# All weight sums of a layer's up projection on Vector instead of GpSimd, with a kept first block, another order of w_o's units and later gate pieces

## The chip, the cores and the metric

The kernel runs on one core of a Trainium2 chip. The metric is the device time of one execution in microseconds (us); the median of the kernel before is 1641.47 us over 3 runs. The engines are TensorE (PE, with its weight loads as PEld), Vector (DVE), Scalar (ACT), GpSimd (POOL) and SyncE (SP), whose queue issues most of the transfers. Each engine runs its instructions in the order of the program.

## The reference

One decoder layer on a sequence of 1024 tokens with 1024 channels, in float32. What matters here is its second half:

```python
x  = LN_1(alpha * x + gate1 * (y @ w_o))                # y: the two mixers, gated
h2 = LN(x) * (1 + scale2) + shift2
u  = h2 @ w_up                                          # 1024 -> 2 * 2816
u  = conv_b + sum(conv_w[t] * pad(u)[:, t:t + S] for t in range(3))   # causal, per channel
f  = gelu(u_gate) * u_val
x  = LN_2(alpha * x + gate2 * (f @ w_down))
```

`gate2` is one part of `SiLU(c) @ w_ada + b_ada`, a vector of 1024 numbers.

## The kernel before, in words

Every float32 operand of a matmul is held as a high and a low part (`hi`, `lo`), and a product is three matmuls (hi*hi, lo*hi, hi*lo). The split is made by two instructions: a CAST on Scalar writes hi (L381), and a subtraction on Vector writes lo (L382). TensorE's order is written by hand. A planner hangs other work between its units: `at(delay, cost, fn)` puts `fn` into a queue, and it is emitted when the planner's clock (in planned us of TensorE work) has passed the delay. The order on each other engine is the order of emission.

The stages, in us of the trace: modulation, first layer norm and the mixers up to about 840; w_o with the two layer norms behind it to about 950; the up projection with its convolution to about 1377; the down projection with the last layer norm to the end.

**w_o.** The work is cut in units `(n, t)`: token tile t of 128 rows, and columns 0-255 (n = 0), 256-511 (n = 1) or 512-1023 (n = 2). A unit is 24 matmuls. Its result goes from PSUM to SBUF by one instruction on Vector, the evacuation (L982). When the last unit of a tile, n = 2, is evacuated, the tile is complete and `ln_tile(t)` follows: `ln_a` is LN_1 (statistics on Vector, L367 and L369; `rs` on GpSimd, L360 and L361; the two passes L1067 and L1068 on Vector), `ln_b` is the statistics of the second norm on Vector, `rs` and `nb` on GpSimd (L360, L361, L377), and the normalisation on Scalar (L1073). Behind tile 3, and again behind tile 7, come eight `h2_part`s each: four transposes on TensorE (L1084), one Scalar pass out of PSUM with the modulation (L1089), then a split into h2's hi and lo.

**The up projection** is done as seven products of blocks instead of eight (Winograd's form of Strassen's rule): h2 is cut in four blocks of 512 tokens by 512 channels, B11, B12, B21 and B22, from which `T1 = B12 - B11`, `T2 = B22 - T1`, `T3 = B22 - B12` and `T4 = B21 - T2` are made on Vector (h2_part, `t1_t3`, `b22_t4`; L1075, L1112, L1115, L1124). The weights come in 22 pairs i of 128 gate channels and 128 value channels. Each pair has four blocks of weights of 128x512 numbers, and four sums of these are made by tensor_tensor instructions: three when `operand` is called for product 6 (L1210 to L1212), one for product 4 (L1216). All four stand on GpSimd:

```python
pool.tensor_tensor(out=r[4], in0=r[2], in1=r[3], op=ALU.add)
pool.tensor_tensor(out=r[2], in0=r[0], in1=r[2], op=ALU.subtract)
pool.tensor_tensor(out=r[0], in0=r[4], in1=r[0], op=ALU.subtract)
```

`operand` is called seven products ahead of its use, and splits the block or sum (names `whi`, `wlo`, from `raw` or `wst`). A product is twelve matmuls (L1265 to L1267) into a bank `pj`, `m` or `w`, and its evacuation adds it to `u` (L1275 on Vector, L1272 a copy on Scalar). Behind a pair's last product come `conv` (L1175 on Scalar, two passes L1177 on Vector, for gate and value each), the GELU (L1184, Scalar), the multiplication (L1185, Vector) and the store to `fd` (SP). The first four pairs run two of their seven products (1 and 2) early, in and between w_o's last units and the transposes.

**The gate.** gate2 is computed on Vector in 36 pieces (`ada3_part`): a load of 128x256 weights and one multiply-add each (L601). The piece number m comes at a planned delay of ADA3_D + ADA3_P * m.

**The down projection** reads `fd` back in 512 columns (`down_prep`), splits it (`fh`, `fl`, or `fe` for the first three blocks) and the weights, and starts with the blocks of `fe` (`f_slot`), which lie in the pool of the convolution's tiles, tag `y`. Its results are evacuated, scaled by gate2 and normalised by `finish`.

Of the kernel before, what the change touches and what calls it, by code (L numbers as in the profile page):

```python
# [9 lines left out]
F32 = mybir.dt.float32  # L10
F32R = mybir.dt.float32r
# [19 lines left out]
PSCALE = 2.0 ** 14  # L31

EARLY = 4
B_FIRST = 3
B_LAST = (3, 5)
MOD_PE = 2
ADA3_D = 70.0
ADA3_P = 8.5
T3_P, T4_P = 2.0, 2.6
ADA_D = 5.0  # L40
ADA_E = 8
# [76 lines left out]
def hybrid_layer_kernel(ctx: ExitStack, tc: tile.TileContext, x, pos, wlra, wbig, wup, wdn, ada1, ada2, cst, pv, sm, lr,  # L118
# [959 lines left out]
    def h2_part(hf, kt):  # L1078

        if h2[hf] is None:  # L1080
            h2[hf] = [hp.tile([P, 4, NK, P], F32R, name=f"h2{hl}", tag="h") for hl in "hl"]
        pt = ps1("m")
        for t in range(4):
            pe.transpose(out=pt[:, t * P:(t + 1) * P], in_=x1[4 * hf + t][:, kt * P:(kt + 1) * P], identity=ident)  # L1084
        if hf == 0:
            f = hq.tile([P, 512], F32, name="xt", tag="raw", bufs=6)
        else:
            f = tmp["b", kt] = t_slot(3 if kt < 4 else 4, "h", kt % 4, F32)
        act.activation(out=f, in_=pt, func=AF.Identity, scale=mods[:, 3][:, kt:kt + 1], bias=mods[:, 2][:, kt:kt + 1])  # L1089
        if hf == 0:  # L1090
            split_to([hl[:, :, kt, :] for hl in h2[0]], rows4(f))
        elif kt < 4:
            t1 = tmp["t1", kt] = t_slot(3, "l", kt, F32)
            b11 = [hl[:, :, kt, :].bitcast(F32) for hl in h2[0]]
            sub(rows4(t1), rows4(f), b11[0])
            sub(rows4(t1), rows4(t1), b11[1])
        else:
            k = kt - 4
            t2 = tmp["t2", k] = t_slot(4, "l", k, F32)
            sub(t2, f, tmp["t1", k])  # L1100
            if k % 2 == 0:
                t2h[0] = hq.tile([P, 2, 512], F32R, name="t2h", tag="t2h", bufs=2)
            tt_[2][k] = t2h[0][:, k % 2, :], t_slot(2, "l", k)
            split_to(tt_[2][k], t2)
# [41 lines left out]
        pe.matmul(pt, lhsT=ones, rhs=gate[:, cs], start=True, stop=True)  # L1146
        act.copy(out=gate[:, cs], in_=pt)

    for n, t in ((2, 0), (1, 4), (2, 1), (1, 5), (2, 2), (1, 6), (2, 3), (1, 7), (2, 4), (2, 5), (2, 6), (2, 7)):
        if n < 2:  # L1150
            wo_unit(n, t)
        else:
            o_unit(t, g_o2, 512, 512, lambda: ln_tile(t))
        if n == 2 and t % 4 == 3:
            for m in range(NK):
                kt = m if t == 3 else m // 2 + 4 * (m % 2)
                at(H2_D + H2_P * m, 0.45, lambda kt=kt, t=t: h2_part(t // 4, kt))
# [35 lines left out]
    def load(i, js=(0, 2, 3, 1)):  # L1193
# [4 lines left out]
            sp.dma_start(r[j], wup[i, j].rearrange("p (k c) -> p k c", k=4))  # L1198
        return r

    def operand(i, p):

        if p < 3 and i < EARLY:
            return pair(load(i, (p - 1,))[p - 1])
        if i not in raws:
            raws[i] = load(i)
        r = raws[i]
        if p == 6:
            r[4] = hq.tile([P, 4, P], F32, name="raw", tag="raw", bufs=6)
            pool.tensor_tensor(out=r[4], in0=r[2], in1=r[3], op=ALU.add)  # L1210
            pool.tensor_tensor(out=r[2], in0=r[0], in1=r[2], op=ALU.subtract)
            pool.tensor_tensor(out=r[0], in0=r[4], in1=r[0], op=ALU.subtract)  # L1212
        if p == 7 and i + 1 < NFF and i + 1 not in raws:
            raws[i + 1] = load(i + 1)
        if p == 4:
            pool.tensor_tensor(out=r[1], in0=r[1], in1=r[0], op=ALU.subtract)  # L1216
        return pair(r[{1: 0, 2: 1, 3: 1, 4: 3, 5: 4, 6: 0, 7: 2}[p]])

    seq = [(0, 1), (1, 1), (0, 2), (1, 2), (2, 1), (3, 1), (2, 2), (3, 2)]
# [64 lines left out]

    def f_slot(s, i):

        if s == 0 and i < B_FIRST:
            e_ = yp.tile([P, 2, 512], F32R, name="fe", tag="y")
            return e_[:, 0, :], e_[:, 1, :]
# [122 lines left out]
```

## Time and profile before

| what | value |
| --- | --- |
| time, median of 3 runs | 1641.47 us (1641.31 to 1641.97) |
| time of the profiled execution | 1640.05 us |
| span of the profiled execution, first to last instruction | 1638.3 us |
| mean granted clock of TensorE in it | 0.987 |
| TensorE busy | 1572.9 us, 96% |
| Vector busy | 1090.7 us, 67% |
| Scalar busy | 746.2 us, 46% |
| GpSimd busy | 470.7 us, 29% |

The span leaves out what lies ahead of the first instruction and behind the last, 1.75 us in this execution. The granted clock is the TensorE clock that the chip allowed, as a share of full speed (2.4 GHz; the lower level is 1.2 GHz), so a stretch at 0.90 ran part of it at the lower level. Busy time is the time in which at least one instruction of the engine runs.

### The profile page before, as it was taken

What the parts mean: (1) busy time and instruction counts of PE and PEld (TensorE: products, weight loads), DVE (VectorE), ACT (ScalarE), POOL (GpSimd) and SP (SyncE); (2) the same over time, 40 slices, a digit from 0 to 9 for tenths busy, and PEclk for the clock granted to TensorE, in tenths of its full rate; (3) what the DMA queues carried; (4) which work ended last, traced back from release to release, by engine and by line L of the source; (5) the groups of instructions that cost most, each with busy time, mean ns of one, the idle gap of its engine ahead of it and who ended that gap; (6) DMA issues with size and microseconds to landing.
All of it is one profiled execution on the core that took longest, in us unless ns stands there. A gap on an engine that the chain in (4) does not pass through costs nothing.

```text
span 1638.3 us, 28077 instructions
## 1 busy us (share of the span) xinstructions
PE 1572.9 (96%) x10542; PEld 1390.8 (85%) x10543; DVE 1090.7 (67%) x2125; ACT 746.2 (46%) x1710; POOL 470.7 (29%) x662
## 2 busy tenths in 40 slices
PE   6999999999999999999999779999999998999997
PEld 5999999998998998989988657778888777888885
DVE  6766666675746555535759799898888877437535
ACT  5665555554544534544423544444444444333430
POOL 2122222222532623515404442333223220003103
PEclk9999999999999999999999889999999999999999
DMA  7500000013114032120244313332222225743641
GB/s 265 159 27 27 28 27 27 28 53 113 60 43 149 26 104 91 31 64 18 65 154 148 104 55 103 105 98 78 77 78 78 79 73 195 250 143 112 203 142 52
DMA packets 79795, 152.87 MB, mean 93 GB/s; under 512 B 8981, under 2 KB 15641, under 8 KB 79658
## 3 DMA queue, kind: packets, MB, share of 16 engines
q1 hardware_dynamic: 79658, 151.07, 28.8%
q8 instruction: 83, 1.36, 0.4%
q14 instruction: 54, 0.44, 0.1%
HBM read 131.11 MB, written 19.92 MB: 92 GB/s over the span
## 4 chain that ended last, share of the span: by engine, by line
PE 79%; DVE 11%; DMA 3%; issue 3%; ACT 2%; POOL 2%; SPq 0%; POOLq 0%; DVEq 0%; ACTq 0%
PE pj L337 10%; PE pj L338 10%; PE pj L339 10%; PE w L1323 7%; PE pj L1323 4%; PE m L1323 3%; PE w L1265 3%; PE w L1267 2%; PE w L1266 2%; DVE cv L1177 2%; PE m L715 2%; PE pj L352 2%; PE m L754 2%; PE pj L353 2%; PE pj L354 2%
## 5 line engine op out<-in xcount | busy, mean ns | idle before, releaser
L337 PE MATMUL pj<-whi,hh 128*128 128x256 f32 (+1 forms) x1296 | 372.6, 287 | 0.1
L339 PE MATMUL pj<-whi,hl 128*128 128x256 f32 (+1 forms) x1296 | 366.2, 283 | 0.0
L338 PE MATMUL pj<-wlo,hh 128*128 128x256 f32 (+1 forms) x1296 | 366.1, 282 | 0.0
L337 PEld LDWEIGHTS pj<-whi,hh 128*128 128x128 f32 x1296 | 247.4, 191 | 0.6 <-issue 0.2
L338 PEld LDWEIGHTS pj<-wlo,hh 128*128 128x128 f32 x1296 | 245.7, 190 | 0.5 <-issue 0.2
L339 PEld LDWEIGHTS pj<-whi,hl 128*128 128x128 f32 x1296 | 245.5, 189 | 0.0
L381 ACT CAST whi<-wst 128x512 fp32r<-128x512 f32 x176 | 107.0, 618 | 150.3 <-PE w L1266 48.4
L382 DVE TENSOR_TENSOR wlo<-wst,whi 128x512 fp32r<-128x512 f32 x176 | 132.5, 763 | 52.4 <-ACT whi L381 52.2
L1177 DVE SCALAR_TENSOR_TENSOR cv<-u,pv_sb,cv 128x1023 f32<-128x1023 f32 x88 | 118.4, 1346 | 10.0 <-ACT cv L1175 10.0
L360 POOL TENSOR_SCALAR rs<-mv 128x1 f32<-128x1 f32 x32 | 15.3, 478 | 329.0 <-DVE mv L1336 245.4
L253 DVE TENSOR_TENSOR wlo<-wst,whi 128x512 fp32r<-128x512 f32 (+1 forms) x108 | 78.1, 742 | 45.7 <-ACT whi L252 45.3
L382 DVE TENSOR_TENSOR fl<-wst,fh 128x512 fp32r<-128x512 f32 x41 | 29.0, 708 | 80.5 <-ACT fh L381 80.5
L381 ACT CAST whi<-raw 128x512 fp32r<-128x512 f32 x66 | 40.9, 620 | 80.3 <-PE m L1266 39.9
L694 POOL TENSOR_SCALAR_AFFINE_SELECT pch<-ph 128x512 f16<-128x512 f16 x32 | 20.5, 642 | 195.5 <-ACT ph L689 195.5
L1210 POOL TENSOR_TENSOR raw<-raw 128x512 f32<-128x512 f32 x22 | 35.5, 1616 | 140.6 <-DMA raw<-in_wup 85.8
L1216 POOL TENSOR_TENSOR wst<-wst 128x512 f32<-128x512 f32 x22 | 36.3, 1651 | 133.4 <-issue 125.4
L252 ACT CAST whi<-wst 128x512 fp32r<-128x512 f32 (+1 forms) x108 | 65.4, 620 | 20.1 <-PE pj L353 10.6
L1265 PE MATMUL pj<-h2h,whi 128*128 128x512 f32 x176 | 71.4, 406 | 1.5 <-DVE y L982 1.5
L1266 PE MATMUL pj<-h2l,whi 128*128 128x512 f32 x176 | 69.9, 397 | 0.0
L1267 PE MATMUL pj<-h2h,wlo 128*128 128x512 f32 x176 | 69.9, 397 | 0.0
L601 DVE SCALAR_TENSOR_TENSOR gate<-aw,csil,gate 128x512 f32<-128x512 f32 (+1 forms) x70 | 57.5, 830 | 17.8 <-DMA aw<-in_ada 17.6
L1266 PE MATMUL m<-h2l,whi 128*128 128x512 f32 x176 | 69.2, 393 | 0.0
(461 smaller groups left out, 4472.2 us busy)
## 6 DMA issues: line engine op xcount, KB each, us to landing
wst<-in_wbig SPq DMA_DIRECT2D x112, 256.0 KB, 3.0
wst<-in_wdn SPq DMA_DIRECT2D x88, 256.0 KB, 3.3
aw<-in_ada SPq DMA_DIRECT2D x80, 256.0 KB, 3.4
wst<-in_wup SPq DMA_DIRECT2D x52, 256.0 KB, 2.6
raw<-in_wup SPq DMA_DIRECT2D x44, 256.0 KB, 2.9
fd<-cv SPq DMA_DIRECT2D x22, 512.0 KB, 4.0
wst<-fd SPq DMA_DIRECT2D x44, 256.0 KB, 3.1
y<-in_x SPq DMA_DIRECT2D x8, 512.0 KB, 8.9
```

The source lines that it names most:

```text
L252: act.copy(out=hi, in_=st)
L253: dve.tensor_tensor(out=lo, in0=st, in1=hi.bitcast(F32), op=ALU.subtract)
L337: pe.matmul(acc, lhsT=lh, rhs=wh, start=kt == 0 if start is None else start, stop=False)
L338: pe.matmul(acc, lhsT=lh, rhs=wl, start=False, stop=False)
L339: pe.matmul(acc, lhsT=ll, rhs=wh, start=False, stop=kt == NK - 1 if stop is None else stop)
L381: act.copy(out=hl[0], in_=src)
L382: dve.tensor_tensor(out=hl[1], in0=src, in1=hl[0].bitcast(F32), op=ALU.subtract)
L1177: dve.scalar_tensor_tensor(out=c_[:, lag:S], in0=u[:, 0:S - lag], scalar=wv[:, 2 - lag:3 - lag], in1=c_[:, lag:S], op0=ALU.mult, op1=ALU.add)
L1265: pe.matmul(acc, lhsT=wh[:, kt, :], rhs=bh, start=p not in (2, 3) and kt == 0, stop=False, **go)
L1266: pe.matmul(acc, lhsT=wh[:, kt, :], rhs=bl, start=False, stop=False, **go)
L1267: pe.matmul(acc, lhsT=wl[:, kt, :], rhs=bh, start=False, stop=kt == 3, **go)
L1323: pe.matmul(acc, lhsT=l_[:, ts_], rhs=r_, start=i == 0 and n == 0, stop=i == NFF - 1 and n == 2)
```

## The change

Five edits, in the order of the diff:

1. All four sums of all 22 pairs are issued on Vector, 88 instructions; GpSimd has none of them.
2. The gate's pieces begin at a planned delay of 130 instead of 70 and follow each other at 7.5 instead of 8.5.
3. For the first four channel blocks, the first half of h2 (B11) is written to slots of its own (tag `t2l`, four slots, later used by T2's low parts) and kept in float32 until T1 is made. T1 is then one subtraction from it; before, it took two, one for B11's high and one for its low part. These four blocks no longer take slots of tag `raw`.
4. The order of w_o's last units.
5. In the down projection's first half the first two blocks `fe` lie in slots of tag `t2h` instead of slots of tag `y`.

```diff
+S_DVE = NFF
...
-ADA3_D = 70.0
-ADA3_P = 8.5
+ADA3_D = 130.0
+ADA3_P = 7.5
...
         if hf == 0:
-            f = hq.tile([P, 512], F32, name="xt", tag="raw", bufs=6)
+            f = (hq.tile([P, 512], F32, name="xt", tag="raw", bufs=6) if kt > 3 else
+                 hq.tile([P, 512], F32, name="t2lf", tag="t2l", bufs=4))
+            tmp["b11", kt] = f
         else:
...
             t1 = tmp["t1", kt] = t_slot(3, "l", kt, F32)
-            b11 = [hl[:, :, kt, :].bitcast(F32) for hl in h2[0]]
-            sub(rows4(t1), rows4(f), b11[0])
-            sub(rows4(t1), rows4(t1), b11[1])
+            sub(t1, f, tmp.pop(("b11", kt)))
...
-    for n, t in ((2, 0), (1, 4), (2, 1), (1, 5), (2, 2), (1, 6), (2, 3), (1, 7), (2, 4), (2, 5), (2, 6), (2, 7)):
+    for n, t in ((2, 0), (2, 1), (2, 2), (1, 4), (2, 3), (1, 5), (2, 4), (1, 6), (2, 5), (1, 7), (2, 6), (2, 7)):
...
+    eng = lambda i: dve if i < S_DVE else pool
+
     def operand(i, p):
...
-            pool.tensor_tensor(out=r[4], in0=r[2], in1=r[3], op=ALU.add)
-            pool.tensor_tensor(out=r[2], in0=r[0], in1=r[2], op=ALU.subtract)
-            pool.tensor_tensor(out=r[0], in0=r[4], in1=r[0], op=ALU.subtract)
+            eng(i).tensor_tensor(out=r[4], in0=r[2], in1=r[3], op=ALU.add)
+            eng(i).tensor_tensor(out=r[2], in0=r[0], in1=r[2], op=ALU.subtract)
+            eng(i).tensor_tensor(out=r[0], in0=r[4], in1=r[0], op=ALU.subtract)
...
         if p == 4:
-            pool.tensor_tensor(out=r[1], in0=r[1], in1=r[0], op=ALU.subtract)
+            eng(i).tensor_tensor(out=r[1], in0=r[1], in1=r[0], op=ALU.subtract)
...
     def f_slot(s, i):
 
+        if s == 0 and i < 2:
+            e_ = hq.tile([P, 2, 512], F32R, name="fe", tag="t2h", bufs=2)
+            return e_[:, 0, :], e_[:, 1, :]
         if s == 0 and i < B_FIRST:
             e_ = yp.tile([P, 2, 512], F32R, name="fe", tag="y")
```

Line numbers of the changed kernel are one higher from the new constant on, two to three higher from `operand` on (L1213 to L1215 and L1219 are the sums, L1278 the evacuation on Vector, L1178 the convolution's passes).

Three places of the program follow as rows of each engine's order.

Vector, from the evacuation of w_o's last unit (2,7) to the second statistics of its tile 7 (`mv<-bst` at the end). Before:

```order
L982 SCALAR_TENSOR_TENSOR y<-xt,pj 128x512
L367 BN_STATS bst<-y 128x6 x3
L369 BN_AGGR mv<-bst 128x2
L367 BN_STATS bst<-y 128x6
L382 TENSOR_TENSOR wlo<-wst,whi 128x512
L369 BN_AGGR mv<-bst 128x2
L601 SCALAR_TENSOR_TENSOR gate<-aw_14571,csil,gate 128x256
L1067 SCALAR_TENSOR_TENSOR y<-y,mv,g1b 128x1024
L1068 SCALAR_TENSOR_TENSOR y<-y,rs,b1b 128x1024
L382 TENSOR_TENSOR wlo<-wst,whi 128x512
L367 BN_STATS bst<-y 128x6 x2
L382 TENSOR_TENSOR wlo<-raw,whi 128x512
```

(the aggregation L369 of tile 7's second statistics is the next row). In the changed kernel:

```order
L983 SCALAR_TENSOR_TENSOR y<-xt,pj 128x512
L368 BN_STATS bst<-y 128x6 x3
L370 BN_AGGR mv<-bst 128x2
L1213 TENSOR_TENSOR raw<-raw 128x512
L1068 SCALAR_TENSOR_TENSOR y<-y,mv,g1b 128x1024
L370 BN_AGGR mv<-bst 128x2
L1214 TENSOR_TENSOR raw<-wst,raw 128x512
L1069 SCALAR_TENSOR_TENSOR y<-y,rs,b1b 128x1024
L1215 TENSOR_TENSOR wst<-raw,wst 128x512
L368 BN_STATS bst<-y 128x6 x2
L383 TENSOR_TENSOR wlo<-wst,whi 128x512
L370 BN_AGGR mv<-bst 128x2
```

Three sums of a pair stand in the chain now, and two splits, one gate piece and the other tile's last statistics row have left it.

GpSimd at the same place, before, where the layer norms' small instructions (`rs`, `nb`) and the sums share one order:

```order
L1210 TENSOR_TENSOR raw<-raw 128x512
L360 TENSOR_SCALAR rs<-mv 128x1
L361 TENSOR_TENSOR rs<-rs,mhalf 128x1
L1211 TENSOR_TENSOR raw<-wst,raw 128x512
L377 TENSOR_SCALAR nb<-mv,rs 128x1
L1212 TENSOR_TENSOR wst<-raw,wst 128x512
L360 TENSOR_SCALAR rs<-mv 128x1
L361 TENSOR_TENSOR rs<-rs,mhalf 128x1
```

In the changed kernel:

```order
L361 TENSOR_SCALAR rs<-mv 128x1
L362 TENSOR_TENSOR rs<-rs,mhalf 128x1
L361 TENSOR_SCALAR rs<-mv 128x1
L362 TENSOR_TENSOR rs<-rs,mhalf 128x1
L378 TENSOR_SCALAR nb<-mv,rs 128x1
```

Only the small ones are left there.

Vector in the up projection, where a pair's products 7, 5 and 4 are evacuated and the next pair's sums are due. Before, one pair's stretch from one evacuation of `m` to the next of `w`:

```order
L1275 TENSOR_TENSOR u<-m,u 128x512
L382 TENSOR_TENSOR wlo<-raw,whi 128x512
L601 SCALAR_TENSOR_TENSOR gate<-aw_15399,csil,gate 128x256
L1275 TENSOR_TENSOR u<-w_14230,u 128x512
L382 TENSOR_TENSOR wlo<-wst,whi 128x512
L601 SCALAR_TENSOR_TENSOR gate<-aw_15463,csil,gate 128x256
L382 TENSOR_TENSOR wlo<-wst,whi 128x512
```

In the changed kernel, some pairs later, where the gate's pieces stand now:

```order
L1278 TENSOR_TENSOR u<-m,u 128x512
L383 TENSOR_TENSOR wlo<-raw,whi 128x512
L1213 TENSOR_TENSOR raw<-raw 128x512
L1278 TENSOR_TENSOR u<-w_14517,u 128x512
L383 TENSOR_TENSOR wlo<-wst,whi 128x512
L1214 TENSOR_TENSOR raw<-wst,raw 128x512
L1215 TENSOR_TENSOR wst<-raw,wst 128x512
L602 SCALAR_TENSOR_TENSOR gate<-aw_15703,csil,gate 128x256
L383 TENSOR_TENSOR wlo<-wst,whi 128x512
```

The first sum L1213, which reads two blocks just loaded, now stands ahead of an evacuation (`u<-w`). On SP a pair's four loads and its store come in the order raw, wst, raw, wst, fd in place of raw, wst, wst, raw, fd.

Scalar between the up and the down projection, up to the cast of the third block `fe`. Before:

```order
L381 CAST fe<-wst 128x512
L381 CAST whi<-wst 128x512 x2
L381 CAST fh<-wst 128x512
L381 CAST whi<-wst 128x512
L1175 ACTIVATE cv<-u,pv_sb 128x1024
L381 CAST whi<-wst 128x512
L381 CAST fh<-wst 128x512
L1175 ACTIVATE cv<-u,pv_sb 128x1024
L381 CAST fe<-wst 128x512
```

In the changed kernel:

```order
L382 CAST fe<-wst 128x512 x2
L382 CAST whi<-wst 128x512
L1275 COPY u<-pj 128x512
L382 CAST whi<-wst 128x512
L1185 ACTIVATE cv<-cv 128x1024
L382 CAST whi<-wst 128x512 x3
L1176 ACTIVATE cv<-u,pv_sb 128x1024
L382 CAST whi<-wst 128x512
L1176 ACTIVATE cv<-u,pv_sb 128x1024
L382 CAST fe<-wst 128x512
```

The first two `fe` are cast together, and the two casts of `fh` that stood ahead of the third are behind it.

## Rows read from the trace of the kernel before

**Rows 1.** The page's first part: busy us, share of the span, instructions.

```profile
PE 1572.9 (96%) x10542; PEld 1390.8 (85%) x10543; DVE 1090.7 (67%) x2125; ACT 746.2 (46%) x1710; POOL 470.7 (29%) x662
```

**Rows 2.** Busy time by stretch: PE, PEld, DVE, ACT, POOL; then clock, DMA share, GB/s.

```profile
852.40:931.60 79.20, 70.20 (x357) 58.00 (x355) 68.15 (x106) 29.05 (x40) 38.85 (x48) 0.97 0.45 148
...
852.40:1000.00 147.60, 126.34 (x572) 101.04 (x571) 132.42 (x189) 64.28 (x94) 59.67 (x59) 0.92 0.33 107
1000.00:1120.00 120.00, 118.34 (x508) 94.64 (x507) 108.58 (x129) 51.76 (x72) 35.73 (x25) 1.00 0.31 102
1120.00:1320.00 200.00, 199.48 (x864) 161.52 (x863) 158.68 (x173) 88.93 (x124) 65.34 (x43) 1.00 0.25 80
...
932.90:994.90 62.00, 49.86 (x198) 38.00 (x196) 59.01 (x79) 32.86 (x53) 18.84 (x10) 0.88 0.18 53
```

**Rows 3.** TensorE's waits from 840 to 1010: us in total, times, longest.

```profile
PE w L1265 <- DVE u L1275: 7.0, 3, 3.3
PE m L1084 <- ACT y L1073: 4.8, 1, 4.8
PE m L1084 <- ACT xt L1089: 2.7, 1, 2.7
PE w L1265 <- ACT t4h L381: 2.2, 1, 2.2
PE w L1266 <- DVE t4l L382: 2.1, 1, 2.1
PE pj L1265 <- DVE y L982: 1.5, 1, 1.5
```

**Rows 4.** TensorE's timeline in w_o: start, us, what; a fast and a slow stretch.

```profile
863.77 0.40 PE L337 MATMUL pj<-t3h,yTh 128*128 128x512 f32 x1
...
904.76 0.63 PE L337 MATMUL pj<-t3h,yTh 128*128 128x512 f32 x1
```

**Rows 5.** Vector's timeline at the first and the last tile of w_o; idle before, releaser.

```profile
852.63 0.69 DVE L982 SCALAR_TENSOR_TENSOR y<-xt,pj 128x512 f32<-128x512 f32 x1 [1.78 <-PE pj L339]
...
914.89 0.68 DVE L982 SCALAR_TENSOR_TENSOR y<-xt,pj 128x512 f32<-128x512 f32 x1
...
923.41 2.31 DVE L1068 SCALAR_TENSOR_TENSOR y<-y,rs,b1b 128x1024 f32<-128x1024 f32 x1 [2.15 <-POOL rs L361]
...
928.03 0.20 DVE L369 BATCH_NORM_AGGREGATE mv<-bst 128x2 f32<-128x12 f32 x1
```

**Rows 6.** GpSimd's timeline at the last tile's second norm.

```profile
928.32 0.94 POOL L360 TENSOR_SCALAR rs<-mv 128x1 f32<-128x1 f32 x1 [3.68 <-DVE mv L369]
```

**Rows 7.** Scalar's timeline, the normalisation of the last tile.

```profile
930.32 1.24 ACT L1073 ACTIVATE y<-y,nb,rs 128x1024 f32<-128x1024 f32 x1 [5.15 <-POOL nb L377]
```

**Rows 8.** Vector's timeline behind the transposes.

```profile
956.15 1.78 DVE L1075 TENSOR_TENSOR xt<-t4hf,t3hf 128x512 f32<-128x512 f32 x1
...
959.56 0.68 DVE L1075 TENSOR_TENSOR xt<-h2h,t4lf 128x512 f32<-128x512 f32 x1
960.16 0.68 DVE L1115 TENSOR_TENSOR t3l<-xt,t3h 128x512 fp32r<-128x512 f32 x1
...
994.27 0.69 DVE L1275 TENSOR_TENSOR u<-w,u 128x512 f32<-128x512 f32 x1
```

**Rows 9.** TensorE's waits from 1000 to 1120.

```profile
PE w L1265 <- DVE u L1275: 1.7, 5, 0.6
```

**Rows 10.** A pair's last load issued by SP, twice, and the sum on GpSimd behind it.

```profile
1174.71 0.33 SPq L1198 DMA_DIRECT2D raw<-in_wup  x1
...
1194.04 0.33 SPq L1198 DMA_DIRECT2D raw<-in_wup  x1
...
1178.45 1.36 POOL L1210 TENSOR_TENSOR raw<-raw 128x512 f32<-128x512 f32 x1 [6.05 <-DMA raw<-in_wup]
```

**Rows 11.** The start of the down projection, Scalar and TensorE.

```profile
1381.62 0.60 ACT L381 CAST fe<-wst 128x512 fp32r<-128x512 f32 x1
...
1382.27 0.80 PE L1323 MATMUL pj<-whi,fe 128*128 128x512 f32 x1 [4.01 <-ACT fe L381]
```

## The prediction

> **What bounds the kernel now.** The page's first part comes first: TensorE is busy for 1572.9 of 1638.3 us, the others far less [rows 1]. So work moved between other engines can gain at most what TensorE loses, about 65 us, and the question is where it loses them and to whom. The busy time by stretch answers the first half. In the convolution's steady part, 1120 to 1320, TensorE is busy 199.48 of 200 us at full clock: nothing is to be gained there. In 1000 to 1120 it loses 1.7 us. From 852.4 to 1000 it is busy 126.34 of 147.6 us and its clock was 0.92 [rows 2]: 21.3 us of waits, and a part of the rest at the lower clock level. This is where the change can act. The view of TensorE's waits names the releasers there: 7.0 us for evacuations on Vector, 4.8 for the normalisation of the last tile on Scalar, 2.7 for the first half's h2 blocks, 2.2 and 2.1 for T4's parts, 1.5 for w_o's last evacuation [rows 3]. The waits are paid twice: a matmul of 512 columns takes 0.40 us before them and 0.63 us behind one [rows 4].
>
> Then I ask what those releasers wait for, and it is Vector each time. From 932.9 to 994.9 Vector is busy 59.01 of 62.0 us, more than TensorE's 49.86 [rows 2]: in this stretch Vector is the bound. Part of that busy time is not its own. The subtraction L1075 on 512 columns took 1.78 us at 956.15, while a sum ran on GpSimd, and 0.68 at 959.56, when none did; alone, such instructions start 0.60 apart [rows 8]. And at w_o's end Vector stood still for 2.15 us until GpSimd had made `rs` [rows 5], which stood behind the sums in GpSimd's order.
>
> **The change part by part.** I sum in four places, from Vector's prices. Unhindered, I count an instruction by the distance of starts: 0.60 us for 512 columns [rows 8], 1.20 for 1024 (twice that), 0.40 for a gate piece and 0.1 for an aggregation (estimates).
>
> *First place, up to the second half's transposes.* From 852.4 until the normalisation ends at 930.32 + 1.24 = 931.6 [rows 7], TensorE is busy 70.2 of 79.2 us at 0.97 of the clock [rows 2]. The idle 9.0 us are the three waits 2.7 + 1.5 + 4.8 [rows 3]; the clock costs 0.03 x 79.2 = 2.4. At full speed without waits TensorE would be there at 931.6 - 9.0 - 2.4 = 920.2. The new unit order puts the units (1,t) between the (2,t), so that tiles complete further apart and the last unit no longer comes as the fourth in a row; I leave 1.5 us of waiting for the blocks in front: 921.7. Does Vector's chain allow that? From its first evacuation (852.63 + 0.6 = 853.2) to the evacuation of (2,7) at 914.89 [rows 5], 61.7 us, the order of before has 86 instructions, 50.7 us unhindered; so 11.0 went to waits and hindrance. The changed order has 85, 50.3 us, since what sums it takes on is offset by gate pieces and splits that went later. I take half of the 11.0, because the hindrance by GpSimd goes and the waits for TensorE stay: 853.2 + 50.3 + 5.5 = 909. From there to tile 7's second aggregation it is 8.7 us with three sums on the way, 1.8 of it; before, it took from 914.89 to 928.03, 13.1 [rows 5], for 9.1 of work. Behind it, GpSimd starts 0.3 us and Scalar 2.3 us later [rows 6, 7]; this remains. So 909 + 8.5 + 2.3 + 1.2 = 921.0, just ahead of TensorE. The gain is 931.6 - 921.7 = **9.9**; the bounds are 0 (the chain stays as late) and 11.4 (no wait, full clock).
>
> *Second place, from there to 995.* Before, Vector needed 62.0 us for 78 instructions up to the evacuation at 994.27 that TensorE awaits [rows 8]. They are 69 of 512 columns, 6 of 1024 and 3 gate pieces: 69 x 0.60 + 6 x 1.20 + 3 x 0.40 = 49.8 us. Ten of them were stretched beyond 0.60 or 1.20 between starts, by 8.6 us together (the row of 956.15 is one: 1.1); the other 3.6 are waits. In the changed order 84 instructions lie in front of that evacuation, 54.8 us: nine sums come (+5.4), the four second subtractions of T1 go (-2.4), a multiplication and a convolution pass that stood behind it now stand in front (+2.4), and a gate piece leaves (-0.4). With the 3.6 of waits, and 1.0 for the sums' waits for their operands, it is 59.4 in place of 62.0. The gain is **2.6**. The bounds: 8.6 of hindrance less 5.0 of work, 3.6, if no new wait arises, and 4.6 more if the old waits go too; and a loss of 5.0, if the hindrance stays or returns as waits.
>
> At this place the Trainium skill (Perfetto Trace Analysis, Optimizing Scalar/DVE Operations) speaks against the change: if DVE is saturated, handing work to Scalar or even GpSimd can make sense, and here work is taken back by a saturated Vector. It adds that the two share a port to SBUF, so that moving work between them might not help. The trace has the first (59.01 of 62.0 us busy) and bears the second out with 1.78 against 0.68 us. By the first alone the second place would lose 5.0, and the time would be near 1634.6; by the second it gains.
>
> *Third place, 1000 to 1120.* TensorE waited 1.7 us, five times, for an evacuation on Vector [rows 9]. There, gate pieces leave (about three per pair went through this stretch) and sums come. I take **1.0**, between 0 and 1.7.
>
> *Fourth place, the start of the down projection.* TensorE waited 4.01 us for the third block's cast, issued at 1381.62 [rows 11]. In the changed order the two casts `fh` stand behind it, and the first two blocks no longer wait for a slot of the convolution's tiles; the cast still waits for a slot and for the convolution's last passes. I take **1.0** and bound it by 0 and 4.0.
>
> *At nothing:* the 88 sums over the rest of the convolution. 18 pairs take 1194.04 - 1174.71 = 19.3 us each [rows 10], set by TensorE. In 1120 to 1320 Vector is busy 158.68 us [rows 2]; with four sums in each of 10.4 pairs, 10.4 x 2.4 = 25, it stays at 184 of 200 at most, and at less as hindrance by GpSimd goes. Gate pieces, about two in a pair for some time, add 0.8 per pair. The cover is TensorE's own 19.3 us; without it each sum would cost 0.6. The later gate is needed only when the first tile of the down projection finishes, some hundred us later. SP's queue issues as many transfers as before.
>
> Sum: 9.9 + 2.6 + 1.0 + 1.0 = 14.5 us. The profiled execution took 1640.05, so 1625.55; the median of the runs shown lies 1.42 higher, which gives **1627.0** us.
>
> **The rivals.**
>
> *Everything hidden by Vector goes* (1614 to 1622). The 5.5, 3.6 and 1.0 us of waits that I left on Vector were partly followers of GpSimd's delays; without them, and with the whole 4.0 at the last place, the gain is 11.4 + 7.2 + 1.7 + 4.0 = 24.3, or 1617. For it: TensorE's waits all hang on one engine, and each wait removed spares lower clock behind it. Against it: the evacuations wait for TensorE as well.
>
> *The first place alone counts* (1632 to 1637). Vector, already the bound behind the transposes, loses with its added work as much as it gains: 9.9 - 5.0 = 4.9, or 1636.6, up to 9.9 and 1631.6 without loss.
>
> *No change* (1638.2 to 1644.8). Three sums stand between the two statistics of the last tile, and each waits for a load. If one is 10 us late, the normalisation is as late as before and the first place gives nothing.
>
> *Slower.* In each pair the first sum stands ahead of the evacuation of `w` in Vector's order and waits for the pair's last load. On GpSimd it began 3.74 us after the issue (1174.71 to 1178.45) [rows 10], where nothing was behind it. Vector's pair without the sums is 7 splits, 5 evacuations and 5 instructions of 1024 columns, 12 x 0.60 + 5 x 1.20 = 13.2 us; with four sums it is 15.6, and with two gate pieces 16.4. Of the 3.74 us I let Vector wait half, 1.9, since it has work in hand for the other half (an estimate). 19.3 - 16.4 - 1.9 = 1.0 is left. So it decides from a landing 4.8 us after issue on; at 6 us each of 18 pairs would be 1.2 us longer, +21.6 against -14.5: 1648.5. Against it: two successive pairs show the same distance, and the changed SP order issues the last `raw` load no later.
>
> **How the numbers follow.** Main case 0.45, with a range of its own of 1622 to 1632; everything goes 0.20; first place alone 0.20; no change 0.08; slower 0.07. A measurement of this kernel can tell about 0.2%, 3.3 us, from no change. Faster by over that holds the first three: 0.85; within it 0.08; slower 0.07. The range of 8 in 10 goes from 1616, which leaves out the lower edge of the second case, to 1637, the upper end of the third: it leaves out the last two cases and a little below.
>
> **What would show it.** First place: the wait for `y` on Scalar in front of the transposes at 1 us or gone, the transposes at about 922, GpSimd's `rs` directly behind the aggregation. Second place: no 512-column instruction on Vector above 0.7 us; the awaited evacuation at about 982. Third: no waits above 0.5 us. Fourth: the wait for `fe` at about 3 us. Steady pairs at 19.3 us, Vector's first sum with a wait of about 2 us. The prediction is wrong if pairs are longer than 19.4, if a sum at w_o's end waits long for its load, or if Vector's waits behind the transposes grow beyond 5 us.

## The result

| what | before | changed |
| --- | --- | --- |
| median of 4 runs | 1641.72 us (1641.31 to 1644.71) | 1624.45 us (1621.93 to 1624.92) |
| profiled execution: time, span | 1640.05, 1638.3 us | 1624.25, 1622.4 us |
| mean granted clock | 0.987 | 0.990 |

The ratio of the times is 0.9888, 95% interval 0.9871 to 0.9905: faster by 17.3 us, where 14.5 us and 1627.0 were forecast. The page's first part of the changed kernel, to be held against [rows 1]:

```profile
PE 1565.8 (97%) x10543; PEld 1388.2 (86%) x10543; DVE 1084.5 (67%) x2209; ACT 745.1 (46%) x1710; POOL 333.6 (21%) x574
```

GpSimd lost 88 instructions and 137 us, Vector gained 84 instructions and yet is busy for 6 us less: its other instructions became shorter by more than the sums cost it. Busy time by stretch, columns as in [rows 2]:

```profile
852.40:921.60 69.20, 68.90 (x351) 57.77 (x351) 61.39 (x103) 25.25 (x35) 26.10 (x38) 0.97 0.47 158
...
1000.00:1120.00 120.00, 120.00 (x521) 97.55 (x520) 105.84 (x146) 54.34 (x75) 0.00 (x0) 1.00 0.28 93
1120.00:1320.00 200.00, 200.00 (x868) 162.73 (x867) 166.81 (x227) 88.37 (x123) 0.00 (x0) 1.00 0.27 87
```

TensorE has next to no idle time in front of the transposes (busy 68.90 of 69.20 us), and none from 1000 to 1320. Its waits from 835 to 1000, columns as in [rows 3]:

```profile
PE w L1268 <- DVE u L1278: 9.2, 3, 5.9
PE w L1268 <- ACT t4h L382: 2.0, 2, 1.8
...
PE m L1085 <- ACT y L1074: 1.2, 1, 1.2
PE w L1269 <- DVE t4l L383: 0.9, 2, 0.6
PE m L1085 <- ACT t4hf L1092: 0.3, 1, 0.3
PE m L1085 <- ACT t2lf L1092: 0.3, 1, 0.3
```

The waits in front of the transposes, 2.7 us for the first half's blocks (the row with `t2lf` now) and 4.8 for `y`, are 0.3 and 1.2 now, and that for w_o's last evacuation is gone. The waits for Vector's evacuations behind the transposes are not shorter but longer, 9.2 in place of 7.0 us, and the longest of all the stage is one of them, 5.9 us.

The last tile's chain: Vector, GpSimd, Scalar, TensorE in the timeline of the changed kernel, to be held against [rows 5 to 7].

```profile
911.79 0.67 DVE L983 SCALAR_TENSOR_TENSOR y<-xt,pj 128x512 f32<-128x512 f32 x1
...
920.60 0.69 DVE L383 TENSOR_TENSOR wlo<-wst,whi 128x512 fp32r<-128x512 f32 x1 [0.82 <-ACT whi L382]
921.21 0.20 DVE L370 BATCH_NORM_AGGREGATE mv<-bst 128x2 f32<-128x12 f32 x1
...
921.50 0.55 POOL L361 TENSOR_SCALAR rs<-mv 128x1 f32<-128x1 f32 x1 [2.71 <-DVE mv L370]
...
923.65 1.24 ACT L1074 ACTIVATE y<-y,nb,rs 128x1024 f32<-128x1024 f32 x1 [2.60 <-POOL nb L378]
...
924.94 0.33 PE L1085 MATMUL m<-ident,y 128*128 128x128 f32 x1 [1.17 <-ACT y L1074]
```

From the evacuation to the second aggregation it took 9.4 us instead of 13.1, with three sums inside, and the transposes came at 924.94 instead of 931.61.

Behind them Vector runs without hindrance. One stretch of its timeline (compare [rows 8]), and TensorE's wait at its end:

```profile
947.99 0.68 DVE L1076 TENSOR_TENSOR xt<-h2h,t4lf 128x512 f32<-128x512 f32 x1
948.59 0.68 DVE L1213 TENSOR_TENSOR raw<-raw 128x512 f32<-128x512 f32 x1
949.19 0.68 DVE L1125 TENSOR_TENSOR xt<-xt,h2l 128x512 f32<-128x512 f32 x1
...
980.36 1.27 DVE L1178 SCALAR_TENSOR_TENSOR cv<-u,pv_sb,cv 128x1022 f32<-128x1022 f32 x1
981.55 1.22 DVE L1186 TENSOR_TENSOR cv<-cv 128x1024 f32<-128x1024 f32 x1
982.69 1.28 DVE L1178 SCALAR_TENSOR_TENSOR cv<-u,pv_sb,cv 128x1023 f32<-128x1023 f32 x1
983.88 0.68 DVE L1278 TENSOR_TENSOR u<-w,u 128x512 f32<-128x512 f32 x1
...
984.62 0.79 PE L1268 MATMUL w<-t3h,whi 128*128 128x512 f32 x1 [5.93 <-DVE u L1278]
985.21 0.63 PE L1269 MATMUL w<-t3l,whi 128*128 128x512 f32 x1
```

Each instruction takes its 0.68 us (or 1.2 to 1.3 for 1024 columns) with 0.60 between starts, the sums too. What TensorE waits for at the end, the evacuation at 983.88, stands behind the convolution of the first two pairs, which nobody awaits yet.

To set the runs side by side, I cut the program at four matmuls that TensorE runs in all of them: the first of the early products (`pj<-h2h,whi`), the last tile's first transpose behind its wait, the start of the third pair's product with T3 (the awaited one above), and the first with `fe`. The spans between these starts, from TensorE's timeline:

| kernel | first product at | to the transposes | to the awaited product | to `fe` | `fe` to the first `w` bank |
| --- | --- | --- | --- | --- | --- |
| before | 911.13 | 20.48 | 63.40 | 381.69 | 11.42 |
| changed | 910.07 | 14.87 | 59.68 | 378.27 | 9.33 |

The differences are 1.1 + 5.6 + 3.7 + 3.4 + 2.1 = 15.9 us, the difference of the whole spans (1638.3 and 1622.4).

### The profile page after: what moved, and what is told of

Same layout as the page of the kernel before. It is cut to its first block, busy times and chain, and to the rows that moved or that the text cites. A ratio compares the mean times of both kernels' runs of the same rounds, so it can differ in the third digit from the quotient of the medians.

```text
span 1622.4 us, 27993 instructions
## 1 busy us (share of the span) xinstructions
PE 1565.8 (97%) x10543; PEld 1388.2 (86%) x10543; DVE 1084.5 (67%) x2209; ACT 745.1 (46%) x1710; POOL 333.6 (21%) x574
## 4 chain that ended last, share of the span: by engine, by line
PE 86%; DVE 7%; DMA 3%; ACT 2%; POOL 1%; issue 1%; SPq 0%; POOLq 0%; DVEq 0%; ACTq 0%
PE pj L338 10%; PE pj L339 10%; PE pj L340 10%; PE w L1329 8%; PE pj L1329 4%; PE w L1268 3%; PE w L1269 3%; PE w L1270 3%; PE m L1329 3%; PE m L1269 2%; PE m L1268 2%; PE m L1270 2%; PE pj L1269 2%; PE pj L1268 2%; PE pj L1270 2%; PE m L716 2%
## 5 line engine op out<-in xcount | busy, mean ns | idle before, releaser
L383 DVE TENSOR_TENSOR wlo<-wst,whi 128x512 fp32r<-128x512 f32 x176 | 121.0, 698 | 36.3 <-ACT whi L382 35.9
L1178 DVE SCALAR_TENSOR_TENSOR cv<-u,pv_sb,cv 128x1023 f32<-128x1023 f32 x88 | 112.3, 1277 | 15.3 <-ACT cv L1176 15.1
L1268 PE MATMUL m<-h2h,whi 128*128 128x512 f32 x176 | 69.1, 392 | 0.0
L1270 PE MATMUL m<-h2h,wlo 128*128 128x512 f32 x176 | 69.0, 392 | 0.0
L672 ACT ACTIVATE ss<-ss,nm 128x128 f32<-128x128 f32 x128 | 49.9, 391 | 39.5 <-DVE nm L669 39.5
L382 ACT CAST fh<-wst 128x512 fp32r<-128x512 f32 x41 | 25.3, 620 | 88.1 <-DMA wst<-fd 87.8
```

The source lines that it names most:

```text
L382: act.copy(out=hl[0], in_=src)
L383: dve.tensor_tensor(out=hl[1], in0=src, in1=hl[0].bitcast(F32), op=ALU.subtract)
L1178: dve.scalar_tensor_tensor(out=c_[:, lag:S], in0=u[:, 0:S - lag], scalar=wv[:, 2 - lag:3 - lag], in1=c_[:, lag:S], op0=ALU.mult, op1=ALU.add)
L1268: pe.matmul(acc, lhsT=wh[:, kt, :], rhs=bh, start=p not in (2, 3) and kt == 0, stop=False, **go)
L1270: pe.matmul(acc, lhsT=wl[:, kt, :], rhs=bh, start=False, stop=kt == 3, **go)
```

## The experiments

Run 1 is the run with the label e1, and so on. Medians are of four runs each. Runs 1 to 4 ran beside a median of before of 1639.78 us, runs 5 to 8 beside 1640.5, runs 9 to 12 beside 1639.77; each ratio is to the kernel before that ran beside it.

**The changed kernel again (e5_changed_again).** No edit.

> The changed kernel once more, as the base for the runs beside it. All theories: 1621 to 1626, and in its trace 14.9 us from the first early product to the last tile's transposes, 59.7 us from there to the awaited product, as in the first trace. What may differ is the stretch ahead of these, where loads of w_o land.

1624.34 us, ratio 0.9905 (0.9886 to 0.9924). The spans were 906.79, 15.51, 60.85, 378.23 and 9.35. So the first product's place alone differed by 3.3 us from the first trace of the same program, and the others by up to 1.2: single traces are read with that in mind, and the medians decide. The base for what follows is 1624.4. The eight runs of the changed kernel, here and in the result, lie between 1621.93 and 1626.49 us; a version whose runs overlap with these is not told apart by its time alone.

**Only the sums (e1_sums_only).** The kernel before with

```diff
-            pool.tensor_tensor(out=r[4], in0=r[2], in1=r[3], op=ALU.add)
+            dve.tensor_tensor(out=r[4], in0=r[2], in1=r[3], op=ALU.add)
...
-            pool.tensor_tensor(out=r[1], in0=r[1], in1=r[0], op=ALU.subtract)
+            dve.tensor_tensor(out=r[1], in0=r[1], in1=r[0], op=ALU.subtract)
```

for all four sums.

> The kernel before with all 88 weight sums on Vector and nothing else changed. Theory (GpSimd's sums stretch Vector's two-operand instructions and hold up the layer norms' small instructions, and that is most of what the change removes): 8 to 12 us faster than before, 1630 to 1634, with no 512-column instruction on Vector above 0.7 us from 932 to 995, and the last tile's normalisation some 4 us earlier. Rival (the new order of w_o's units, which spreads the tiles' ends, brings the first place's gain): at most 4 us faster, or slower, since Vector only gets more work.

1632.48 us, ratio 0.9950 (0.9935 to 0.9965), 7.3 us faster than the kernel before beside it: a little under the theory's range, well above the rival's. Its waits of TensorE from 830 to 1120:

```profile
PE w L1265 <- DVE u L1275: 9.6, 3, 5.9
PE m L1084 <- ACT xt L1089: 2.8, 1, 2.8
...
PE m L1084 <- ACT y L1073: 1.0, 1, 1.0
```

The last tile's wait is 1.0 as in the changed kernel, without any new order: 15.01 us from the first product to the transposes. The wait of 2.8 ahead of them is the order's part. And from the transposes to the awaited product it took 64.01 us, where before took 63.40 and the same program's two traces differ by 1.2: no gain is seen there, Vector's added work ate what it gained.

**All but the sums (e2_all_but_sums).** The changed kernel with

```diff
-S_DVE = NFF
+S_DVE = 0
```

> The changed kernel with all sums back on GpSimd; order, kept block, later gate pieces and fe slots stay. Theory: 9 to 13 us slower than the changed kernel, 1633 to 1637, with the stretched instructions back. Rival: within 4 us of the changed kernel, 1624 to 1629, as order, kept block and gate take the load off Vector.

1633.98 us, ratio 0.9957 (0.9941 to 0.9974), so the sums are worth 9.6 us in the changed kernel; the rival falls. Vector's groups between the transposes and the awaited product in this run, then two of the same groups in the changed kernel (count, busy, mean ns of one):

```profile
L383 DVE TENSOR_TENSOR wlo<-wst,whi 128x512 fp32r<-128x512 f32 x5 | 5.0, 991 | 0.0
...
L1178 DVE SCALAR_TENSOR_TENSOR cv<-u,pv_sb,cv 128x1023 f32<-128x1023 f32 x3 | 4.6, 1519 | 0.9 <-ACT cv L1176 0.9
```

```profile
L1178 DVE SCALAR_TENSOR_TENSOR cv<-u,pv_sb,cv 128x1023 f32<-128x1023 f32 x4 | 5.1, 1276 | 0.0
...
L383 DVE TENSOR_TENSOR wlo<-wst,whi 128x512 fp32r<-128x512 f32 x6 | 4.1, 681 | 1.0 <-ACT whi L382 1.0
```

With sums on GpSimd the split takes 991 ns on average, without them 681. At w_o's end, two rows of Vector's timeline in run 2:

```profile
915.67 2.31 DVE L1068 SCALAR_TENSOR_TENSOR y<-y,mv,g1b 128x1024 f32<-128x1024 f32 x1
...
922.76 1.28 DVE L1069 SCALAR_TENSOR_TENSOR y<-y,rs,b1b 128x1024 f32<-128x1024 f32 x1 [3.34 <-POOL rs L362]
```

Both ways of hindering stand here side by side: a pass takes 2.31 us where it took 1.27 in the changed kernel, and Vector idles 3.34 us for `rs`, which stood behind four sums in GpSimd's order. No run separates the two at this place. The spans: 21.29 us to the transposes (6.4 more than the changed kernel), 60.89 to the awaited product (1.2 more), 381.92 to `fe` (3.7 more).

**The old order of w_o's units (e3_old_order).**

```diff
-    for n, t in ((2, 0), (2, 1), (2, 2), (1, 4), (2, 3), (1, 5), (2, 4), (1, 6), (2, 5), (1, 7), (2, 6), (2, 7)):
+    for n, t in ((2, 0), (1, 4), (2, 1), (1, 5), (2, 2), (1, 6), (2, 3), (1, 7), (2, 4), (2, 5), (2, 6), (2, 7)):
```

> The changed kernel with w_o's last units in the order of before. Theory: 2 to 4 us slower than the changed kernel: the waits of 2.7 and 1.5 us come back in front of the first transposes and at the last evacuation, the last tile's normalisation is late by that. Rival (the order is what counts): 8 us or more slower, 1632 and up.

1628.0 us, ratio 0.9924 (0.9909 to 0.9939): 3.6 us slower in the median, as the theory has it; the fastest of its four runs, 1626.14, just overlaps with the slowest of the changed kernel's. The trace has the wait for the first half's blocks back, 2.9 us, while the last tile's stays at 1.1. From the first product to the transposes it took 16.58 us, 1.7 more than the changed kernel.

**The sums of the first four pairs only (e4_first_four_pairs).**

```diff
-S_DVE = NFF
+S_DVE = EARLY
```

> The changed kernel with the sums of the first four pairs on Vector and those of the other 18 on GpSimd, as before. Theory (the sums matter where Vector is the bound, up to about 1000, and in the convolution TensorE covers them): within 2 us of the changed kernel, at most 1626.5; if anything slower by the waits of 0.3 to 0.6 us per pair between 1000 and 1120. Rival (the steady pairs on GpSimd cost as much as the first ones): 5 us or more slower.

1628.87 us, ratio 0.9929 (0.9914 to 0.9944): 4.4 us slower than the changed kernel, between the theory's 2 us and the rival's 5. Of the 9.6 us of the sums, nearly half come from the 18 pairs of the convolution, which I had put at nothing but for one us; in the trace the span from the awaited product to `fe` is 383.82 us, 5.5 more than in the changed kernel. Busy time by stretch in this run, and its waits from 990 to 1120:

```profile
1000.00:1120.00 120.00, 117.08 (x502) 93.66 (x501) 106.97 (x125) 51.38 (x72) 36.09 (x24) 1.00 0.30 97
1120.00:1320.00 200.00, 199.60 (x862) 161.24 (x862) 160.82 (x176) 88.63 (x123) 63.34 (x41) 1.00 0.24 81
```

```profile
PE w L1268 <- DVE u L1278: 2.9, 5, 0.9
```

In the same 120 us TensorE ran 502 matmuls here and 521 in the changed kernel. The idle time shows 2.9 us; 19 matmuls at some 0.23 us are 4.4. What the waits hide can be read at one of them, in TensorE's timeline of the kernel before:

```profile
1095.25 0.39 PE L1267 MATMUL m<-h2h,wlo 128*128 128x512 f32 x1
1096.19 0.50 PE L1265 MATMUL w<-t4h,whi 128*128 128x512 f32 x1 [0.55 <-DVE u L1275]
1096.53 0.40 PE L1266 MATMUL w<-t4l,whi 128*128 128x512 f32 x1
1096.76 0.39 PE L1267 MATMUL w<-t4h,wlo 128*128 128x512 f32 x1
```

Matmuls start 0.23 us apart and are listed with 0.39, so they overlap. Across the wait the starts are 0.94 and then 0.34 apart, 0.71 + 0.11 = 0.82 us more than usual, where 0.55 is listed; from the next one on it is 0.23 again. So a short wait costs some 0.27 us beyond its listed time, and five of them 1.4 more than the 2.9. From 1120 on the loss is smaller, 862 matmuls instead of 868, some 1.4 us.

**Idle copies on GpSimd (e6_idle_copies_on_gpsimd).** The changed kernel with

```diff
             eng(i).tensor_tensor(out=r[0], in0=r[4], in1=r[0], op=ALU.subtract)
+            for _ in range(4):
+                pool.tensor_tensor(out=r[3], in0=r[3], in1=ones.unsqueeze(1).to_broadcast([P, 4, P]), op=ALU.mult)
```

> The changed kernel, in which GpSimd additionally multiplies one block of each pair by ones, four times per pair (88 instructions of 128x512), behind Vector's sums. Values and Vector's work stay; GpSimd reads SBUF and its queue holds work again. Theory (it is GpSimd's reading that stretches Vector): 6 to 12 us slower than the changed kernel, stretched instructions of 1.1 to 1.8 us on Vector again, and waits of 0.2 to 0.6 us in the convolution's pairs. Rival (the sums were only in the wrong place in GpSimd's order or took too long there): within 2 us of the changed kernel, since nothing that Vector needs soon hangs on these copies.

1688.67 us, ratio 1.0298 (1.0282 to 1.0313): 64 us slower than the changed kernel, 48 slower than before. The mechanism is the theory's, its size is five times the 12 us that I expected at most. Vector's groups from 1120 to 1320 and the time by stretch:

```profile
L383 DVE TENSOR_TENSOR wlo<-wst,whi 128x512 fp32r<-128x512 f32 x37 | 31.6, 854 | 0.0
...
L1214 DVE TENSOR_TENSOR raw<-wst,raw 128x512 f32<-128x512 f32 x10 | 17.8, 1782 | 0.0
L1215 DVE TENSOR_TENSOR wst<-raw,wst 128x512 f32<-128x512 f32 x9 | 16.0, 1780 | 0.0
...
L602 DVE SCALAR_TENSOR_TENSOR gate<-aw,csil,gate 128x256 f32<-128x256 f32 x10 | 9.9, 994 | 0.0
...
L1280 DVE TENSOR_TENSOR u<-w,u 128x512 f32<-128x512 f32 x27 | 18.5, 684 | 5.7 <-PE w L1272 5.7
```

```profile
1120.00:1320.00 200.00, 184.12 (x755) 146.50 (x754) 181.18 (x205) 76.89 (x108) 56.72 (x38) 0.96 0.23 77
```

The copies start when the first sum on Vector is done, and the instructions that Vector has next are just those with two operands in SBUF: two sums at 1.78 instead of 0.68 us, a split, a gate piece. That is 1.1 + 1.1 + 0.8 + some 0.5 = 3.5 us per pair, on top of 16.4 for the work and some 2 for waits: over the 19.3 us of a pair. Vector became the bound of every pair: the twelve pairs from the seventh's to the nineteenth's T3 product take 266.07 us instead of 232.79, 2.8 more each. Of the 64 us, 17.8 arise ahead of the awaited product (1002.37 in place of 984.62) and 45.8 from there to `fe`. No engine is listed as waiting for GpSimd from 985 to 1400, so in the convolution it is the stretch and not GpSimd's order that costs the time. Some 2 us of hindrance per pair cost 0.2 us in the kernel before, on average over these pairs (235.26 against 232.79); 3.5 us cost 2.8 when Vector carries the sums: it is not the stretch alone but the slack that it meets. The case is that of the slower rival, Vector as the bound of each pair, reached by another way than a late load and at more than its 1.2 us per pair.

**The gate at its old times (e7_old_gate).**

```diff
-ADA3_D = 130.0
-ADA3_P = 7.5
+ADA3_D = 70.0
+ADA3_P = 8.5
```

> The changed kernel with the gate's pieces at the planned times of before (70 and 8.5 in place of 130 and 7.5). Theory: 0 to 2 us slower than the changed kernel, by waits of TensorE for evacuations between 1000 and 1120, where Vector would be some 5 us fuller. Rival (the gate pieces in w_o's end are what held the last tile up): 3 us or more slower, the last tile's normalisation late by more than 2 us.

1624.31 us, ratio 0.9902 (0.9887 to 0.9917): no difference. TensorE was busy all of 1000 to 1120 without the later gate as well:

```profile
1000.00:1120.00 120.00, 120.00 (x521) 97.56 (x520) 105.90 (x145) 54.28 (x76) 0.00 (x0) 1.00 0.29 93
```

**The block not kept (e8_block_not_kept).**

```diff
-            sub(t1, f, tmp.pop(("b11", kt)))
+            b11 = [hl[:, :, kt, :].bitcast(F32) for hl in h2[0]]
+            sub(rows4(t1), rows4(f), b11[0])
+            sub(rows4(t1), rows4(t1), b11[1])
```

with `f` in a `raw` slot again.

> The changed kernel with B11 not kept in float32: T1 takes two subtractions in four blocks, 2.4 us of Vector's work in the stretch in which Vector is the bound. Theory (that stretch goes at Vector's speed): 2 to 5 us slower than the changed kernel, since its waits also cost clock. Rival (Vector has slack again without hindrance): within 1 us.

1627.84 us, ratio 0.9926 (0.9912 to 0.9941): 3.5 us slower, for 2.4 us of Vector's work. From the transposes to the awaited product it took 62.68 us, 3.0 more than in the changed kernel's first trace and 1.8 more than in its second. So Vector's time there is TensorE's time. What the blocks' return to `raw` slots had in it is not separated.

**The old slots of fe (e9_old_fe_slots).**

```diff
-        if s == 0 and i < 2:
-            e_ = hq.tile([P, 2, 512], F32R, name="fe", tag="t2h", bufs=2)
-            return e_[:, 0, :], e_[:, 1, :]
```

> The changed kernel with the first two blocks fe in the slots of the convolution's tiles again. Theory (the slots and the order of casts behind them are what shortened the start of the down projection from 11.4 to 9.3 us): 11 us or more there, and 1.5 to 2.5 us slower than the changed kernel. Rival (that start hangs on when the last fd lands and is read back; the run with only the sums moved had 9.7 us with the old slots): 9.3 to 10 us, no difference in the time.

1624.55 us, ratio 0.9912 (0.9895 to 0.9928): no difference. The start of the down projection took 10.31 us, short of the theory's 11 and just above the rival's range; with the new slots it was between 9.2 and 10.3 in the traces of this study (7.7 in one), with the old ones 9.7 (run 1) to 11.4 (before). No gain of the slots is shown.

**Putting off the convolution (three runs).** The wait of 5.9 us left open whether a better version lies near. In the changed kernel the first two pairs' convolution was handed to the planner, with a delay:

```diff
             if p == 3:
-                hidden(i, *us.pop(i))
+                u_ = us.pop(i)
+                if i < 2:
+                    at(8.0, 0.0, lambda: hidden(i, *u_))
+                else:
+                    hidden(i, *u_)
```

> The changed kernel, with the convolution of the first two pairs put off by 8 planned us, so that on Vector the evacuations of the third pair stand ahead of it. Theory (from 925 to 985 Vector is behind by about 6 us of work, part of which nobody awaits yet): the wait of 5.9 us at 978.7 goes, and with it the slow matmuls behind it; 4 to 8 us faster than the changed kernel, 1616 to 1620. Rival (Vector's work is only shifted, and the wait comes back one or two products later): within 2 us of the changed kernel.

With `4.0 + 5.0 * i` and with `4.0` as the delay:

> As the run with 8 us, but put off by 4 us for the first and 9 us for the second pair, so that the passes lie between the evacuations in smaller pieces. Theory: also 4 to 8 us faster than the changed kernel; better than 8 and 8 if a bunch of passes there stops an evacuation again. Rival: within 2 us of the changed kernel.

> As the run with 8 us, but with 4 us for both pairs: three passes and a multiplication still stand ahead of the awaited evacuation, about 4.8 us instead of some 8. Theory: about half of the gain of the run with 8 us, 2 to 4 us. Rival: within 2 us of the changed kernel.

8 us later: 1628.99 us (0.9935, 0.9920 to 0.9950), 4.4 slower than run 9 beside it. 4 and 9: 1621.58 (0.9890, 0.9875 to 0.9905), runs from 1620.75 to 1621.96. 4: 1622.72 (0.9896, 0.9881 to 0.9911), runs from 1620.51 to 1624.03. TensorE's waits from 905 to 1020, one line from each of the three:

```profile
PE w L1268 <- DVE u L1278: 13.4, 4, 8.8
```

```profile
PE w L1268 <- DVE u L1278: 7.8, 4, 3.4
```

```profile
PE w L1268 <- DVE u L1278: 6.6, 4, 2.5
```

In all three the wait at the third pair's first product fell from 5.9 to 1.2 or 1.3 us, and a new one came some 25 us later, behind the passes put off: 8.8 us where they were put off as a bunch, 3.4 and 2.1 where they were spread. From the last tile's transposes to the seventh pair's T3 product it took 140.17 us with 8, 132.40 with 4 and 9 and 132.08 with 4, against 134.18 and 135.31 in the changed kernel's two traces and 136.02 in run 9. So both views had a part: most of Vector's arrears are only shifted, but in small pieces between evacuations they cost less. In the median the two better versions are 3.0 and 1.8 us faster than run 9, short of the 4 to 8 and the 2 to 4 expected; 8 us later came out on the other side of both its theory and its rival. The four runs of 4 and 9 (up to 1621.96) lie below the changed kernel's eight (from 1621.93) but for 0.03 us, though the intervals of the ratios overlap (0.9875 to 0.9905 here, 0.9886 to 0.9924 in run 5). The runs of 4 overlap with the changed kernel's: its gain is seen in the trace and not shown by the time.

## Why the prediction was right, and where it was off

In the trace the four terms measure 8.6, 3.7, 3.4 and 2.1 us, together 17.8 where 14.5 were forecast, and 1.9 us of a late start ahead of them leave the 15.9 of the spans. The first term was too high, the others too low: that the total came out nearer than some of them is in part luck.

**What bounds the kernel** held: most of the gain lies where [rows 2] had TensorE waiting, and Vector was what it waited for.

**First place (forecast 9.9).** Counted as forecast, from the end of unit (2,0), it is 8.6 us: that unit ended at 852.4 before and at 854.3 in the changed trace, the transposes at 931.6 and 924.9. In the second trace it is 8.4. It is made of two things that I had in one sum: the order (3.6 us by the medians of run 3) and GpSimd's leaving (6.4 us from the first product to the transposes by the trace of run 2, 5.5 by that of run 1). The chain went as worked out, each link a little later: evacuation 911.8 (forecast 909), aggregation 9.4 behind it (8.5, with 0.8 of waiting for a cast), normalisation 2.4 behind that. (The 8.5 was put into the sum where 8.7 had been worked out.) TensorE's waits, 0.3 + 1.2, are the 1.5 us that I left. The 2.4 us of clock did not come back whole; the start of this stretch in the changed trace:

```profile
854.30:862.00 7.70, 7.70 (x30) 6.16 (x29) 6.85 (x10) 2.48 (x4) 2.18 (x2) 0.86 0.63 204
```

That is some 1.1 us (0.14 x 7.7) at the lower level, behind a wait of 1.2 us at 850.75; from 862 on the clock is 1.00. What the forecast lacked besides is that the stretch ahead of it, where w_o's loads land, shifts by 2 to 3 us from run to run.

**Second place (forecast 2.6).** From the transposes it is 3.7, in the second trace 2.6. My sum of 54.8 us of work and 4.6 of waits was 59.4; Vector took from 927.73 (its first T3 subtraction) to 983.88 + 0.68, 56.8 us, so its waits were 2.0. Part of that it lost again at its start, 2.8 us behind the transposes instead of 1.3. Of the edits, the kept block is worth 3.5 us (run 8). The sums by themselves gain nothing there that the traces could show: 64.01 us against 63.40 in run 1, and 60.89 with them back on GpSimd in run 2, against 59.68 and 60.85. In run 1 the work taken back and the hindrance gone cancel: neither the loss of 5.0 that I had weighed came, nor a gain by the sums alone.

The Trainium skill (Perfetto Trace Analysis, Optimizing Scalar/DVE Operations) has the reservation that moving work between these two engines might not help; at this place run 1 agrees, with 64.01 us against 63.40.

On TensorE the gain of this place does not show as shorter waits:

```profile
931.60:995.00 63.40, 51.15 (x200) 39.10 (x200) 59.27 (x80) 33.73 (x53) 18.84 (x10) 0.87 0.18 55
```

```profile
924.94:984.60 59.66, 47.25 (x200) 35.78 (x200) 56.99 (x88) 35.84 (x57) 0.00 (x0) 0.93 0.24 75
```

Before (first row) and changed it idles some 12.3 us; the same 200 matmuls took 47.25 us in place of 51.15, at a clock of 0.93 in place of 0.87. Where Vector is the bound, TensorE only follows, and the length of Vector's order is what counts.

The Trainium skill (SBUF — State Buffer, Who interferes with whom) states that a DVE instruction with two SBUF inputs contends with a GpSimd instruction that reads SBUF, and that one with at most one such input, outside the 2-port modes, doesn't. Runs 2 and 6 agree: splits went to 0.99 us on average in run 2 and sums to 1.78 in run 6, and the evacuations, which read one operand from PSUM, stayed at 0.68 in both.

**Third place and the rest of the convolution (forecast 1.0 and nothing).** This is the term that was mis-sized. It measured 3.4 in the trace, and 4.4 in the medians (run 4). I read the waits of [rows 9], 1.7 us, as the whole loss and took a part. Five waits at some 0.27 us beyond what is listed make it 3.1, and the matmuls agree: 508 before and 521 changed in these 120 us, 13 at 0.23 us, 3.0. "Nothing is to be gained" in the steady part was nearly right: 864 and 868 matmuls in 1120 to 1320, some 0.9 us, most of it at one wait of 0.52 us at 1305.63. The sums are what makes the loss, as run 4 has it back with GpSimd's sums in the 18 pairs alone. It is not the gate's doing, as I had argued for 1000 to 1120: run 7 has no such wait at the old times.

**Fourth place (forecast 1.0).** The trace shows 2.1, and TensorE's waits for `fe` fell from 4.0 + 0.2 to

```profile
PE pj L1329 <- ACT fe L382: 2.0, 1, 2.0
PE pj L1329 <- DVE fe L383: 1.0, 1, 1.0
```

But run 9 gives the same time and run 1 most of the gain without the edit. That the term had the right sign is luck: the cause I gave is not borne out; what made the start of the down projection long in the trace of before stays open. Over the traces with the new slots the span is spread from 7.7 to 10.3, more than the gain.

**The sums at nothing**: the pairs stay at 19.4 us (232.79 / 12) with Vector's added work, as forecast. In the changed kernel the first sum waits less than the 1.9 us that I set, 11.1 us over ten pairs:

```profile
L1213 DVE TENSOR_TENSOR raw<-raw 128x512 f32<-128x512 f32 x10 | 6.9, 692 | 11.1 <-DMA raw<-in_wup 5.9 <-issue 3.5 <-DVE wlo L383 1.8
```

A late load was not tried, so that way to the slower rival stays untested.

By the medians of single edits undone, 9.6 (sums) + 3.6 (order) + 3.5 (block) + 0 (gate) + 0.2 (slots) = 16.9, against 16.2 for all of them beside run 5: the parts add up within a few us of uncertainty, and nothing large is left to explain.

**Rivals.** "The first place alone counts" and "no change" fell by the time. "Everything hidden by Vector goes" fell with the wait of 5.9 us: Vector is still behind.

## What to carry to other kernels

Work on an engine with time to spare is not free if its reads stretch the instructions of the engine that others wait for: compare the same instruction's duration with and without the neighbour, multiply by the count, and set that against the work's own price on the busy engine (here 2.4 us of sums per pair against some 2 of hindrance, plus the delays in the neighbour's queue). A short wait costs more than its listed idle time, here some 0.27 us more, so that 1.7 us of waits in 120 were a loss of 3.0: count the matmuls, not the busy time. And when an engine is in arrears, look at what in its order nobody awaits yet; move it in small pieces, for put off as a bunch it only moves the wait.

## What was not expected of the hardware

The stretch of a hindered instruction was much the same however it came about: a 512-column instruction on Vector with two operands in SBUF took 1.78 us beside GpSimd's sums and 1.78 beside its multiplications (1.59 us each), 0.68 alone. And whether it costs anything depended on the slack: some 2 us of it per pair cost 0.2 us in the kernel before, where Vector was busy 158.68 of 200 us with it; 3.5 us per pair cost 2.8 where Vector was busy 166.81 of 200 without it. Behind the wait of 5.93 us TensorE's matmuls were slower, 0.63 us at 985.21 where 0.40 is usual, and the granted clock of the stretch was near the lower level:

```profile
984.60:990.00 5.40, 5.38 (x13) 4.24 (x14) 5.19 (x8) 1.34 (x2) 0.00 (x0) 0.54 0.24 96
```
